# mLSTM exponents from broadcast row parts and a ScalarE bias, with the row work spread over small steps

## The chip, the cores and the metric

The kernel runs on one core of one Trainium2 chip. The metric is the device time of one execution in microseconds (us), the median over runs; the profile of one further execution tells where the time went. The engines of the core work in parallel, each through its own queue in order: TensorE (PE in the rows; PEld is its weight load), VectorE (DVE), ScalarE (ACT), GpSimd (POOL) and SyncE (SP), which starts DMA transfers here.

## The reference, cut to what matters

One encoder layer over 2048 tokens of width 1024: three token mixers (a bidirectional mLSTM with 4 heads, a neighbourhood attention, a cross-attention into 256 memory tokens), sigmoid gates that merge them, an output projection, and an MLP of width 4096. All of it is float32. The part that the change touches is the chunk step of the mLSTM, run once forwards and once on the flipped sequence:

```python
b = jnp.cumsum(lf, axis=-1)                       # lf: log of the forget gate
d_log = jnp.where(tril, b[..., :, None] - b[..., None, :] + ig[..., None, :], -jnp.inf)
inter = b + m_st[..., None]
m_t = jnp.maximum(inter, jnp.max(d_log, axis=-1))
s = jnp.einsum('bhtd,bhsd->bhts', q, k) * jnp.exp(d_log - m_t[..., None])
w_inter = jnp.exp(inter - m_t)
num = s @ v + w_inter[..., None] * (c_st @ q)     # shortened
den = jnp.sum(s, axis=-1) + w_inter * (n_st @ q)
h = num / jnp.maximum(jnp.abs(den), jnp.exp(-m_t))[..., None]
```

followed by the update of the state `c_st`, `n_st`, `m_st`. Afterwards the two directions are added, normalised per head and multiplied by a gate `og`. The exponent `d_log - m_t` is a sum of a part that hangs on the column s alone, `a = ig - b`, and a part that hangs on the row t alone, `r = b - m_t`; above the diagonal its exponential is zero.

## The kernel before, in words

The program has three phases. Phase 1 projects the input and runs the attention branches, phase 2 runs the mLSTM beside the gate products, phase 3 does the merge, the output projection and the MLP. The projections are made as three float32 passes over a high and a low part of both operands (`mm3`, L232 to L234), which makes TensorE the busiest engine. TensorE's instructions run in the order in which the code emits them; the other engines' queues are ordered by the scheduler from dependencies and priorities. All DMAs are started from the SP queue.

Phase 2 (`phase_2`, `late_gates`) emits 48 gate groups. One is 24 matmuls into one `mm` buffer of PSUM (there are two), over weights `ws` split by ScalarE (L176, high part) and VectorE (L177, low part); ScalarE evicts it with a Tanh. After each sixth matmul `tick()` lets the generator `ml_stream` (L623) run one step, so a gate group has four ticks. The stream idles for `START_2` = 20 ticks and then goes in slots of four ticks. The slots alternate between direction 0 (chunks 0 to 15) and direction 1 (15 to 0); a chunk is 128 tokens (64 in the reference; the sum is the same). Each slot starts one chunk of its direction (`ml_chunk`) and steps up to four that are under way, by the table `when`. A chunk's first step starts its loads; the next makes the decay matrix `de`; then come scores, state update, denominators, `h`, and in the second half of each direction the normalisation and the transposes for the output.

Ahead of each four chunks of a direction stands `ml_block`, in one piece: it loads the gate rows `ig` and `lf` of 512 tokens for 4 heads from DRAM, forms the running sum (L749) and the running maximum (L753) by two scans on VectorE, then `a`, `r`, the decay `w` (stored to DRAM), and four transposes of the maximum on TensorE (L772) whose exponential `em` is needed for the denominator. Heads lie on 4 partitions per direction (0 to 3 and 32 to 35). For the exponents, `a` and `r` are split into a rounded high part (ScalarE copies, L759 and L762) and a low part (VectorE, L760 and L763), kept in `at` and `rp`.

Per chunk, GpSimd spreads `rp` over the four heads with a 0/1 pattern `bd` (L806, into `rd`); one TensorE product of `at` and `rd` gives a + r for 4 heads x 128 x 128 in PSUM (L809, into a buffer of the pool `mx`); ScalarE takes its exponential as `de` in one pass (L811), and GpSimd masks it. The scores (L827, two `mx` buffers) are multiplied with `de` to `pt` on VectorE (L829) and copied to `sk` on ScalarE (L831), for the other direction's later use; the keys are transposed (L838, `mx`) and weighted to `kw` (L844), `qw` is made on GpSimd (L848), the state update uses one `mx` buffer (L871, read by `C`, L877), the denominators are taken at L882, and the output transposes at L904 use one more (read by `hm`, L907). The PSUM of phase 2 is two `mm`, four `pn` and two `mx` buffers; a tag without a pool of its own, as `tr`, comes out of `mx`.

## Time and profile before

| | |
|---|---|
| median of 3 runs (lowest to highest) | 2985.45 us (2985.35 to 2986.06) |
| the profiled execution's own time, its span | 2988.64 us, 2986.9 us |
| busy: TensorE, VectorE, ScalarE, GpSimd | 97%, 69%, 40%, 8% of the span |
| mean granted TensorE clock | 0.995 |
| HBM traffic over the span | 211 GB/s |

The times of the engines overlap. The span runs from the first to the last instruction of the profiled execution, and the view in order of time counts from its start. Idle time of an engine that is not the one the others wait for costs nothing; idle time of TensorE in a stretch lengthens it. Phase 2 lies roughly between 965 and 1365 us.

### The profile page before, as it was taken

What the parts mean: (1) busy time and instruction counts of PE and PEld (TensorE: products, weight loads), DVE (VectorE), ACT (ScalarE), POOL (GpSimd) and SP (SyncE); (2) the same over time, 40 slices, a digit from 0 to 9 for tenths busy, and PEclk for the clock granted to TensorE, in tenths of its full rate; (3) what the DMA queues carried; (4) which work ended last, traced back from release to release, by engine and by line L of the source; (5) the groups of instructions that cost most, each with busy time, mean ns of one, the idle gap of its engine ahead of it and who ended that gap; (6) DMA issues with size and microseconds to landing.
All of it is one profiled execution on the core that took longest, in us unless ns stands there. A gap on an engine that the chain in (4) does not pass through costs nothing.

```text
span 2986.9 us, 41900 instructions
## 1 busy us (share of the span) xinstructions
PE 2910.6 (97%) x15028; PEld 2374.8 (80%) x15028; DVE 2070.4 (69%) x3557; ACT 1195.1 (40%) x2198; POOL 237.1 (8%) x389
## 2 busy tenths in 40 slices
PE   8999999999999899999999999999999999999999
PEld 6778788878877677778888888888878888888887
DVE  6676775567654765674769888666676888885666
ACT  6454654344543333342233333543312433344331
POOL 3020210011000322330000000000000000000000
PEclk9999999999999999999999999999999999999999
DMA  8776777867799667789535444766874444466655
GB/s 276 225 253 202 231 227 240 266 217 217 240 283 307 195 199 234 240 276 315 183 110 169 155 152 155 275 191 224 268 235 128 137 155 151 154 226 225 195 182 165
DMA packets 341712, 632.97 MB, mean 212 GB/s; under 512 B 29344, under 2 KB 151008, under 8 KB 341504
## 3 DMA queue, kind: packets, MB, share of 16 engines
q1 hardware_dynamic: 341504, 630.30, 65.4%
q8 instruction: 118, 1.93, 0.3%
q14 instruction: 90, 0.74, 0.1%
HBM read 453.63 MB, written 176.55 MB: 211 GB/s over the span
## 4 chain that ended last, share of the span: by engine, by line
PE 55%; DVE 2%; DMA 2%; issue 1%; ACT 0%; POOL 0%; SPq 0%; DVEq 0%; ACTq 0%; POOLq 0%
PE mm L232 18%; PE mm L234 18%; PE mm L233 18%; PE mm L1339 0%; DVE h L900 0%; DMA og<-s_o 0%; DMA wr<-in_w_units_dram 0%; DMA hf<-s_hf 0%; DVE ev L1495 0%; ACT hf L896 0%; POOL rs L325 0%; DVE acc L1488 0%; DVE ws L177 0%; DVE h L888 0%; DMA X<-s_a 0%
## 5 line engine op out<-in xcount | busy, mean ns | idle before, releaser
L232 PE MATMUL mm<-X,ws 128*128 128x512 f32 x1152 | 448.5, 389 | 0.0
L234 PE MATMUL mm<-X,ws 128*128 128x512 f32 x1152 | 448.2, 389 | 0.0
L233 PE MATMUL mm<-X,ws 128*128 128x512 f32 x1152 | 448.1, 389 | 0.0
L232 PE MATMUL mm<-hT,ws 128*128 128x512 f32 x896 | 375.6, 419 | 12.1 <-ACT cz L654 5.5
L177 DVE TENSOR_TENSOR ws<-wr,ws 128x1024 fp32r<-128x1024 f32 (+1 forms) x212 | 263.0, 1246 | 142.8 <-ACT ws L176 137.7
L234 PE MATMUL mm<-hT,ws 128*128 128x512 f32 x896 | 353.6, 395 | 0.0
L233 PE MATMUL mm<-hT,ws 128*128 128x512 f32 x896 | 353.4, 394 | 0.0
L233 PE MATMUL mm<-X 128*128 128x512 f32 x896 | 348.8, 389 | 2.5 <-DVE X L1462 2.5
L234 PE MATMUL mm<-X 128*128 128x512 f32 x896 | 348.7, 389 | 0.5 <-DVE X L1462 0.5
L232 PE MATMUL mm<-X 128*128 128x512 f32 x896 | 348.7, 389 | 0.4 <-ACT X L1461 0.4
L1461 ACT ACTIVATE X<-X 128x1024 fp32r<-128x1024 f32 x176 | 187.0, 1063 | 319.4 <-DMA X<-s_t 124.5
L1462 DVE TENSOR_TENSOR X<-X 128x1024 fp32r<-128x1024 f32 x176 | 214.3, 1224 | 132.8 <-ACT X L1461 132.0
L176 ACT ACTIVATE ws<-wr 128x1024 fp32r<-128x1024 f32 (+1 forms) x212 | 223.5, 1059 | 164.7 <-PE mm L234 91.8
L232 PE MATMUL mm<-ws,hT 128*128 128x512 f32 (+2 forms) x704 | 260.9, 371 | 9.3 <-ACT cz L654 5.1
L234 PEld LDWEIGHTS mm<-X,ws 128*128 128x128 f32 x1152 | 216.2, 188 | 45.1
L233 PEld LDWEIGHTS mm<-X,ws 128*128 128x128 f32 x1152 | 216.2, 188 | 44.9
L232 PEld LDWEIGHTS mm<-X,ws 128*128 128x128 f32 x1152 | 216.2, 188 | 44.5
L234 PE MATMUL mm<-ws,hT 128*128 128x512 f32 (+2 forms) x704 | 249.8, 355 | 1.1 <-DVE hT L434 1.1
L233 PE MATMUL mm<-ws,hT 128*128 128x512 f32 (+2 forms) x704 | 249.0, 354 | 0.3 <-DVE ws L177 0.3
L202 ACT ACTIVATE ws<-wr 128x512 fp32r<-128x512 f32 x224 | 135.3, 630 | 219.9 <-PE mm L234 139.3
L232 PEld LDWEIGHTS mm<-hT,ws 128*128 128x128 f32 x896 | 170.2, 190 | 54.1 <-issue 9.8
L234 PEld LDWEIGHTS mm<-hT,ws 128*128 128x128 f32 x896 | 169.6, 189 | 39.0
(266 smaller groups left out, 4855.3 us busy)
## 6 DMA issues: line engine op xcount, KB each, us to landing
wr<-in_w_units_dram SPq DMA_DIRECT2D x308, 512.0 KB
s_s<-u SPq DMA_DIRECT2D x32, 1024.0 KB
X<-s_s SPq DMA_DIRECT2D x64, 512.0 KB
X<-s_t SPq DMA_DIRECT2D x64, 512.0 KB
s_g<-ev SPq DMA_DIRECT2D x96, 256.0 KB
ev<-s_g SPq DMA_DIRECT2D x96, 256.0 KB
s_a<-u SPq DMA_DIRECT2D x96, 256.0 KB
X<-s_a SPq DMA_DIRECT2D x48, 512.0 KB
```

Source lines behind the costliest of these rows:

```text
L176: nc.scalar.activation(w[:, 0], raw, AF.Copy)
L177: nc.vector.tensor_tensor(w[:, 1], raw, w[:, 0].bitcast(F32), ALU.subtract)
L202: nc.scalar.activation(hi, src, AF.Copy)
L232: mm(out, lhs[0], rhs[0], start=first, stop=False)
L233: mm(out, lhs[0], rhs[1], start=False, stop=False)
L234: mm(out, lhs[1], rhs[0], start=False, stop=last)
L1461: nc.scalar.activation(hi, src, AF.Copy)
L1462: nc.vector.tensor_tensor(lo, src, hi.bitcast(F32), ALU.subtract)
```

## The change

The product of `at` and `rd` is gone, with the constants `bd`, `at`, `rd`, `rp`, the high and low parts and GpSimd's L806. The row part `r` is stored to DRAM (`s_r`) and loaded again, per chunk, as one row of 4 x 128 numbers copied to all 128 partitions (`rb`, 262 KB). The column part `a` is transposed on TensorE beside the maximum (eight transposes per block and direction in place of four) and copied by VectorE to `ac`; ScalarE forms `de` in four passes of 128 columns, one per head, with `ac` as the bias.

`ml_block` becomes the generator `ml_rows(n)`, which treats both directions' block n together. Its rows are one fixed set of five tiles for all blocks; `a`, `r` and the exponential of `w` take both directions in one instruction over 36 partitions. It goes one step per tick: loads, four empty ticks, four ticks with a scan each, one for `a`, `r` and the store of `r`, one for `w`, and one for each direction's transposes. Block 0's begins at tick 8 of the 20 (`ROWS_2`), those of blocks 1 to 3 at the slots 3, 11 and 19; a block's first chunks are due at the slots 8, 16 and 24.

```diff
@@ ml_stream
-        for _ in range(START_2):
+        rows = self.ml_rows(0)
+        for tick in range(START_2):
+            if tick >= ROWS_2:
+                next(rows, None)
             yield
...
-            if c is not None and c % 4 == (0, 3)[d]:
-                self.ml_block(d, c // 4)
+
+            if slot % 8 == 3 and slot < 24:
+                rows = self.ml_rows(slot // 8 + 1)
+            slot += 1
...
+                next(rows, None)
                 yield
@@ ml_consts
...
-        self.packs = []
+        self.pack = [t("r_" + x, [36, TB + 2 * (x == "m")]) for x in "ifbmw"]
@@ ml_block / ml_rows
+        for d, b, hs in dirs:
+            for x, name in ((lf, "lf"), (ig, "ig")):
+                nc.sync.dma_start(x[hs], self.scr[name][4 * d:4 * d + 4, b * TB:(b + 1) * TB])
+        for _ in range(4):
+            yield
+        for d, _, hs in dirs:
+            nc.vector.tensor_tensor_scan(rev(d, bs[hs]), self.reset[hs], rev(d, lf[hs]), 0.0, ALU.mult, ALU.add)
+            yield
...
         nc.vector.tensor_tensor(a, ig, bs, ALU.subtract)
-        nc.scalar.activation(at[hs], a, AF.Copy)
-        nc.vector.tensor_tensor(at[lo], a, at[hs].bitcast(F32), ALU.subtract)
         nc.vector.tensor_tensor(r, bs, cm, ALU.subtract)
-        nc.scalar.activation(rp[hs].bitcast(F32R), r, AF.Copy)
-        nc.vector.tensor_tensor(rp[lo], r, rp[hs], ALU.subtract)
...
+        for d, b, hs in dirs:
+            self.store(self.scr["r"][d][b].rearrange("c h t -> h c t"), r[hs].rearrange("h (c t) -> h c t", t=128))
+        yield
...
+        for d, b, hs in dirs:
+            yield
+            p = self.ps("mx", (128, 4, 128))
+            for c in range(4):
+                for x, col in ((cm, 0), (a, 4)):
+                    nc.tensor.transpose(p[:, c, col:col + 4], x[hs, c * 128:(c + 1) * 128], self.ident[hs, hs])
+            em, ac = self.row(f"r_em{d}", (128, 4, 4)), self.row(f"r_a{d}", (128, 4, 4))
+            nc.scalar.activation(em, p[:, :, 0:4], AF.Exp, scale=-1.0)
+            nc.vector.tensor_copy(ac, p[:, :, 4:8])
@@ ml_chunk
-        rd = self.rd[d, c % 2]
+
+        rb = self.t(f"rb{d}", [128, 4, 128], 2)
+        nc.sync.dma_start(rb, self.scr["r"][d][b][cc].unsqueeze(0).to_broadcast([128, 4, 128]))
...
-        nc.gpsimd.tensor_tensor(rd[64:100], self.bd, R["rp"][:, cs].unsqueeze(1).to_broadcast([36, 4, 128]), ALU.mult)
-        yield
-        pd = self.ps("mx", (128, 4, 128))
-        nc.tensor.matmul(pd, R["at"][:, cs], rd, start=True, stop=True)
+        yield
         de = self.t(f"de{d}", [128, 4, 128], 1)
-        nc.scalar.activation(de, pd, AF.Exp)
+        for h in range(4):
+            nc.scalar.activation(de[:, h], rb[:, h], AF.Exp, bias=R["ac"][:, cc, h:h + 1])
```

What this does to the queues is shown at three places; the numbers at the ends of names tell one use of a buffer from another. First TensorE's queue at an early chunk, from the exponents' product to the scores; `mm` is a gate group's buffer. Before:

```order
L809 MATMUL mx_11143<-rd_10774,at_10773 128x512
L232 MATMUL mm_11130<-hT,ws_10898 128x512
L233 MATMUL mm_11130<-hT,ws_10898 128x512
L234 MATMUL mm_11130<-hT,ws_10898 128x512
L232 MATMUL mm_11130<-hT,ws_10898 128x512
L233 MATMUL mm_11130<-hT,ws_10898 128x512
L234 MATMUL mm_11130<-hT,ws_10898 128x512
L827 MATMUL mx_11155<-qk_1953_11054 128x128
L827 MATMUL mx_11156<-qk_1953_11054 128x128
L827 MATMUL mx_11155<-qk_1953_11054 128x128
L827 MATMUL mx_11156<-qk_1953_11054 128x128
```

and after (the scores' line is now L825):

```order
L232 MATMUL mm_11100<-hT,ws_10868 128x512
L233 MATMUL mm_11100<-hT,ws_10868 128x512
L234 MATMUL mm_11100<-hT,ws_10868 128x512
L232 MATMUL mm_11100<-hT,ws_10868 128x512
L233 MATMUL mm_11100<-hT,ws_10868 128x512
L234 MATMUL mm_11100<-hT,ws_10868 128x512
L825 MATMUL mx_11126<-qk_1952_11044 128x128
L825 MATMUL mx_11127<-qk_1952_11044 128x128
L825 MATMUL mx_11126<-qk_1952_11044 128x128
L825 MATMUL mx_11127<-qk_1952_11044 128x128
```

The product ahead of the gate matmuls has gone; the gate matmuls and the scores keep their order.

Second, TensorE's queue at the chunk in whose scores the first transposes of a later block now follow. Before, six gate matmuls follow the scores:

```order
L233 MATMUL mm_11354<-hT,ws_10997 128x512
L234 MATMUL mm_11354<-hT,ws_10997 128x512
L827 MATMUL mx_11403<-qk_1988_11245 128x128
L827 MATMUL mx_11404<-qk_1988_11245 128x128
L827 MATMUL mx_11403<-qk_1988_11245 128x128
L827 MATMUL mx_11404<-qk_1988_11245 128x128
L232 MATMUL mm_11354<-hT,ws_10997 128x512
L233 MATMUL mm_11354<-hT,ws_10997 128x512
L234 MATMUL mm_11354<-hT,ws_10997 128x512
L232 MATMUL mm_11354<-hT,ws_10997 128x512
L233 MATMUL mm_11354<-hT,ws_10997 128x512
L234 MATMUL mm_11354<-hT,ws_10997 128x512
```

and after, where `r_m` is the running maximum and `r_i` holds `a`:

```order
L825 MATMUL mx_11401<-qk_1986_11222 128x128
L825 MATMUL mx_11402<-qk_1986_11222 128x128
L825 MATMUL mx_11401<-qk_1986_11222 128x128
L825 MATMUL mx_11402<-qk_1986_11222 128x128
L769 MATMUL mx_11411<-ident,r_m 128x4
L769 MATMUL mx_11411<-ident,r_i 128x4
L769 MATMUL mx_11411<-ident,r_m 128x4
L769 MATMUL mx_11411<-ident,r_i 128x4
L769 MATMUL mx_11411<-ident,r_m 128x4
L769 MATMUL mx_11411<-ident,r_i 128x4
L769 MATMUL mx_11411<-ident,r_m 128x4
L769 MATMUL mx_11411<-ident,r_i 128x4
```

The eight transposes moved in directly behind the four score matmuls, alternating between the two row tiles.

Third, VectorE's queue where the second block's row work begins; `ws` is the low part of a weight unit, `r_b` and `r_m` are the scans' outputs, `pt` and `kw` belong to chunks. Before:

```order
L829 TENSOR_TENSOR pt_1968_11154<-mx_11155,de_1967_11145 128x2x128
L829 TENSOR_TENSOR pt_1968_11154<-mx_11156,de_1967_11145 128x2x128
L749 SCALAR_TENSOR_TENSOR r_b_11647<-reset,r_f_11646 4x512
L844 TENSOR_TENSOR kw_1972_11176<-mx_11171,de_1967_11145 128x256
L753 SCALAR_TENSOR_TENSOR r_m_11648<-r_f_11646,r_m_11648,r_i_11645 4x512
L177 TENSOR_TENSOR ws_11126<-wr_11125,ws_11126 128x8x128
L754 COPY carry<-r_m_11648 4x1
L758 TENSOR_TENSOR r_i_11645<-r_i_11645,r_b_11647 4x512
L749 SCALAR_TENSOR_TENSOR r_b_11647<-reset,r_f_11646 4x512
L761 TENSOR_TENSOR r_b_11647<-r_b_11647,r_m_11648 4x512
L760 TENSOR_TENSOR at_10783<-r_i_11645,at_10783 4x512
L829 TENSOR_TENSOR pt_1982_11220<-mx_11221,de_1981_11211 128x2x128
```

and after:

```order
L742 SCALAR_TENSOR_TENSOR r_b<-reset,r_f 4x512
L177 TENSOR_TENSOR ws_11055<-wr_11054,ws_11055 128x8x128
L742 SCALAR_TENSOR_TENSOR r_b<-reset,r_f 4x512
L748 SCALAR_TENSOR_TENSOR r_m<-r_f,r_m,r_i 4x512
L749 COPY carry<-r_m 4x1
L748 SCALAR_TENSOR_TENSOR r_m<-r_f,r_m,r_i 4x512
L827 TENSOR_TENSOR pt_1966_11125<-mx_11126,de_1965_11113 128x2x128
L827 TENSOR_TENSOR pt_1966_11125<-mx_11127,de_1965_11113 128x2x128
L749 COPY carry<-r_m 4x1
L751 TENSOR_TENSOR r_i<-r_i,r_b 36x512
L752 TENSOR_TENSOR r_b<-r_b,r_m 36x512
L759 TENSOR_TENSOR r_w<-r_b,r_m 4x512
```

The four scans moved from behind that chunk's `pt` to ahead of it, and the low part of a weight unit now stands between the first and the second.

## Rows read from the trace of the kernel before

**Rows 1.** The page's engine totals: busy us (share of span) x instructions.

```profile
PE 2910.6 (97%) x15028; PEld 2374.8 (80%) x15028; DVE 2070.4 (69%) x3557; ACT 1195.1 (40%) x2198; POOL 237.1 (8%) x389
```

**Rows 2.** Busy us by engine in stretches; then granted clock, DMA share, GB/s.

```profile
1000.00:1040.00 40.00, 31.20 (x142) 24.29 (x141) 29.03 (x35) 16.25 (x30) 18.32 (x12) 0.92 0.60 189
1034.00:1042.00 8.00, 7.53 (x31) 6.13 (x31) 6.52 (x12) 4.36 (x10) 1.06 (x2) 0.61 0.54 181
1080.00:1120.00 40.00, 37.11 (x221) 27.03 (x221) 28.41 (x54) 16.25 (x37) 11.84 (x15) 1.00 0.57 185
1160.00:1200.00 40.00, 37.67 (x232) 27.63 (x233) 29.18 (x59) 12.96 (x31) 12.14 (x17) 1.00 0.76 260
1200.00:1240.00 40.00, 38.83 (x223) 29.58 (x220) 26.39 (x57) 15.40 (x56) 16.81 (x25) 1.00 0.76 236
1240.00:1280.00 40.00, 38.00 (x219) 28.82 (x219) 27.16 (x59) 14.28 (x47) 14.54 (x23) 1.00 0.81 248
1280.00:1320.00 40.00, 38.30 (x221) 29.18 (x220) 29.81 (x69) 16.28 (x57) 15.81 (x21) 1.00 0.91 279
1320.00:1360.00 40.00, 37.78 (x199) 29.99 (x198) 25.13 (x58) 18.58 (x65) 7.54 (x12) 1.00 0.83 260
```

**Rows 3.** TensorE in order of time: start us, us, instruction, count.

```profile
1000.87 0.39 PE L234 MATMUL mm<-hT,ws 128*128 128x512 f32 x1
1001.19 0.41 PE L772 MATMUL mx<-ident,r_m 4*128 4x4 f32 x4
...
1001.86 0.40 PE L233 MATMUL mm<-hT,ws 128*128 128x512 f32 x1
...
1016.61 0.40 PE L809 MATMUL mx<-rd,at 100*128 100x512 f32 x1
1016.84 0.40 PE L232 MATMUL mm<-hT,ws 128*128 128x512 f32 x1
```

**Rows 4.** Order of time, all engines, 1024 to 1035; [idle before, released by].

```profile
1024.70 1.21 DVE L749 TENSOR_TENSOR_SCAN r_b<-reset,r_f 4x512 f32<-4x512 f32 x1 [4.54 <-DMA r_f<-s_lf]
...
1026.28 0.71 PE L827 MATMUL mx<-qk 64*128 64x128 f32 x8 [1.09 <-DVE kw L844]
...
1029.19 1.59 POOL L806 TENSOR_TENSOR rd<-bd,rp 36x512 fp32r<-36x512 f32 x1
1029.69 2.17 DVE L749 TENSOR_TENSOR_SCAN r_b<-reset,r_f 4x512 f32<-4x512 f32 x1
...
1033.57 0.76 DVE L829 TENSOR_TENSOR pt<-mx,de 128x256 f32<-128x256 f32 x2
...
1034.47 0.69 PE L838 MATMUL mx<-ident,qk 128*128 128x128 f32 x2 [5.89 <-ACT sk L831]
```

**Rows 5.** Groups around the mLSTM stage: busy us, mean ns, idle before.

```profile
L811 ACT ACTIVATE de<-mx 128x512 f32<-128x512 f32 x32 | 18.9, 592 | 28.2 <-PE mx L809 26.4 <-issue 1.6
L896 ACT ACTIVATE hf<-h 128x128 f32<-128x128 f32 x64 | 19.0, 300 | 26.1 <-DVE h L893 26.1
L806 POOL TENSOR_TENSOR rd<-bd,rp 36x512 fp32r<-36x512 f32 x32 | 44.9, 1406 | 56.4 <-PE mx L809 30.2 <-DVE rp L763 25.6
L772 PE MATMUL mx<-ident,r_m 4*128 4x4 f32 x32 | 3.2, 203 | 0.0
```

**Rows 6.** TensorE's waits, 1200 to 1360: us in total, times, longest us.

```profile
PE mx L871 <- DVE hm L907: 3.5, 6, 1.4
PE mx L809 <- ACT sm L882: 0.7, 1, 0.7
PE tr L904 <- DVE C L877: 0.6, 1, 0.6
```

**Rows 7.** The page's costliest groups: the two halves of a weight unit.

```profile
L177 DVE TENSOR_TENSOR ws<-wr,ws 128x1024 fp32r<-128x1024 f32 (+1 forms) x212 | 263.0, 1246 | 142.8 <-ACT ws L176 137.7
L176 ACT ACTIVATE ws<-wr 128x1024 fp32r<-128x1024 f32 (+1 forms) x212 | 223.5, 1059 | 164.7 <-PE mm L234 91.8
```

**Rows 8.** DMA queue, 960 to 1400: packets, MB, share of 16 engines.

```profile
q1 hardware_dynamic: 90450, 105.91, 74.6%
```

More of the change, by code (lines that the diff above doesn't have):

```diff
@@ L305, in scratch @@
             w=[[d(f"s_w{i}{b}", [4, TB]) for b in range(NB)] for i in range(2)],
+            r=[[d(f"s_r{i}{b}", [4, 4, 128]) for b in range(NB)] for i in range(2)],
             hm=[d(f"s_hm{b}", [128, 2, 4, TB]) for b in range(NB)],
@@ L623, in ml_stream @@
     def ml_stream(self):
-        for _ in range(START_2):
+        rows = self.ml_rows(0)
+        for tick in range(START_2):
+            if tick >= ROWS_2:
+                next(rows, None)
             yield
+        slot = 0
         dirs = [list(range(16)), list(range(15, -1, -1))]
@@ L735, in ml_logsig, with ml_rows @@
         self.store(view(self.scr["lf"]), l)
-    def ml_block(self, d, b):
+    def ml_rows(self, n):
         nc = self.nc
-        n = b if d == 0 else 3 - b
-        hs = slice(32 * d, 32 * d + 4)
-        if d == 0:
-            self.packs.append({x: self.row("r_" + x, (36, TB + (x == "m")), bufs=1) for x in "ifbmw"})
-        P = {x: y[hs] for x, y in self.packs[n].items()}
-        ig, lf, bs, m, w = (P[x] for x in "ifbmw")
-        nc.sync.dma_start(ig, self.scr["ig"][4 * d:4 * d + 4, b * TB:(b + 1) * TB])
-        nc.sync.dma_start(lf, self.scr["lf"][4 * d:4 * d + 4, b * TB:(b + 1) * TB])
-        rev = (lambda x: x[:, ::-1]) if d else (lambda x: x)
-        nc.vector.tensor_tensor_scan(rev(bs), self.reset[hs], rev(lf), 0.0, ALU.mult, ALU.add)
-        cm, ce = (m[:, 1:], m[:, 0:1]) if d == 0 else (m[:, :TB], m[:, TB:])
-        carry = self.carry[hs]
-        nc.vector.tensor_copy(ce, carry)
-        nc.vector.tensor_tensor_scan(rev(cm), rev(lf), rev(ig), ce, ALU.add, ALU.max)
-        nc.vector.tensor_copy(carry, m[:, TB:] if d == 0 else m[:, 0:1])
-        lo = slice(32 - 32 * d, 36 - 32 * d)
-        at, rp = self.at[d, n % 2], self.rp[d, n % 2]
-        a, r = ig, bs
@@ new lines, in ml_rows @@
+        ig, lf, bs, m, w = self.pack
+        cm, a, r = m[:, 1:TB + 1], ig, bs
+        dirs = [(d, n if d == 0 else 3 - n, slice(32 * d, 32 * d + 4)) for d in range(2)]
+        rev = lambda d, x: x[:, ::-1] if d else x
+        for d, b, hs in dirs:
[6 more added lines that the diff above has]
+            yield
@@ L758, in ml_block @@
+        for d, _, hs in dirs:
+            ce = m[hs, 0:1] if d == 0 else m[hs, TB + 1:TB + 2]
+            carry = self.carry[hs]
+            nc.vector.tensor_copy(ce, carry)
+            nc.vector.tensor_tensor_scan(rev(d, cm[hs]), rev(d, lf[hs]), rev(d, ig[hs]), ce, ALU.add, ALU.max)
+            nc.vector.tensor_copy(carry, m[hs, TB:TB + 1] if d == 0 else m[hs, 1:2])
+            yield
         nc.vector.tensor_tensor(a, ig, bs, ALU.subtract)
-        nc.scalar.activation(at[hs], a, AF.Copy)
@@ L768, in ml_block @@
-        nc.scalar.activation(w, w, AF.Exp)
-        self.store(self.scr["w"][d][b], w)
-        p = self.ps("mx", (128, 4, 128))
-        for c in range(4):
-            nc.tensor.transpose(p[:, c, 0:4], cm[:, c * 128:(c + 1) * 128], self.ident[hs, hs])
-        em = self.row(f"r_em{d}", (128, 4, 4))
-        nc.scalar.activation(em, p[:, :, 0:4], AF.Exp, scale=-1.0)
-        self.rows[d, b] = dict(at=at, rp=rp, em=em)
+        for d, b, hs in dirs:
+            self.store(self.scr["r"][d][b].rearrange("c h t -> h c t"), r[hs].rearrange("h (c t) -> h c t", t=128))
@@ new lines, in ml_rows @@
+        yield
+        for d, _, hs in dirs:
+            ms = (m[hs, 0:TB] if d == 0 else m[hs, 2:TB + 2]).rearrange("p (c t) -> p c t", t=128)
+            ms = ms[:, :, 0:1] if d == 0 else ms[:, :, 127:128]
+            nc.vector.tensor_tensor(w[hs].rearrange("p (c t) -> p c t", t=128), r[hs].rearrange("p (c t) -> p c t", t=128),
+                                    ms.to_broadcast([4, 4, 128]), ALU.add)
+        nc.scalar.activation(w, w, AF.Exp)
+        for d, b, hs in dirs:
+            self.store(self.scr["w"][d][b], w[hs])
@@ new lines, in ml_rows @@
+        for d, b, hs in dirs:
+            yield
[6 more added lines that the diff above has]
+            nc.vector.tensor_copy(ac, p[:, :, 4:8])
+            self.rows[d, b] = dict(em=em, ac=ac)
```

24 lines of the change are left out of this document (3 added, 21 removed).

## The prediction

> **What bounds the kernel now.** I read the engine totals first, then the stage that the change touches, cut into 40 us pieces, then the waits and the order of time at the places where TensorE stands still. TensorE is busy for 97% of the span [rows 1], so time is won only by taking work from it or by closing a gap in it. The mLSTM stage fills the pieces of rows 2, 1000 to 1360, and some 30 us ahead of them: 32 chunk steps (16 chunks, two directions) woven into the gate products. The pieces show where TensorE stands: 40.00 - 31.20 = 8.8 us in 1000 to 1040, 2.9 in 1080 to 1120, 2.3 in 1160 to 1200, and 1.2 + 2.0 + 1.7 + 2.2 = 7.1 in 1200 to 1360. The first three pieces are the ones in which the row work of a new block of four chunks is done (`ml_block`). In 1034 to 1042 the granted clock is 0.61: after the long stop TensorE ran for a while at the lower of its two levels, 1.2 instead of 2.4 GHz, which cost 8.0 x 0.39 = 3.1 us more.
>
> The longest stop in order of time [rows 4]: the DVE runs block 1's row work from 1024.70 on, first a sum scan of 1.21 us; the score matmuls of L827 wait 1.09 us for the `kw` queued behind it; then row work holds the DVE until `pt` (L829) starts at 1033.57. `pt` frees one of the two `mx` buffers in PSUM, and L838, which needs one, starts at 1034.47 after 5.89 us idle. This is VectorE's queue, not TensorE's work.
>
> **The change, part by part.**
>
> TensorE's work. One matmul per chunk (L809) goes. From its start to the next start is 16.84 - 16.61 = 0.23 us [rows 3] (its 0.40 us overlaps the next): 32 x 0.23 = **-7.4 us**, all of it on the path. The row transposes double: per block and direction 4 more for `a`. Around today's four, L234 at 1000.87 and L233 at 1001.86 are 0.99 us apart [rows 3], where two steps of about 0.23 would be 0.46, so four cost 0.53. Most of that is the change to another kind of matmul and back; four in a row take 0.41 from first start to last end with 0.20 for one (L772 in rows 5), so a further one costs about 0.07. The eight groups get 4 x 0.07 = 0.28 each, **+2.2 us** (no less; up to 8 x 0.53 = 4.2 if alternating between the two row tiles costs like a new group). Together **-5.2**.
>
> Block 0 and block 1. The first block's rows are now worked from tick 8 on and no longer pass through ScalarE twice, and its transposes stand two ticks earlier; the gate evictions that queued behind those ScalarE copies go through. In VectorE's new order block 1's row work starts earlier, but three of its four scans still stand behind a weight half (`ws_11055`) and ahead of chunk 0's `pt`. I time that from the end of the gate group whose eviction precedes that weight half on ScalarE: eviction 0.59 (the 128x512 pass of L811 [rows 5]), weight copy 1.06 and lower half 1.25 [rows 7], three scans at 1.21 [rows 4] = 3.6, and from the start of `pt` to L838 34.47 - 33.57 = 0.90 [rows 4]: 7.4 us. TensorE has 24 matmul steps of 0.23 and the scores, 0.71 [rows 4], before it needs the buffer: 6.2. So I expect a stop of 1.2, and with about 0.1 a piece for three hand-overs **1.5 us**; bounds 0 and today's 5.9. A stop of that size did not lower the clock: 1080 to 1120 has 2.9 us idle and a clock of 1.00 [rows 2]. So 8.8 + 3.1 becomes 1.5: **-10.4**.
>
> The same scan that takes 1.21 us took 2.17 at 1029.69, while GpSimd ran L806 (from 1029.19, 1.59 us) [rows 4]. The Trainium skill, "SBUF — State Buffer", section "Who interferes with whom", says that VectorE and GpSimd lock a shared port: an instruction of VectorE with two SBUF inputs and one of GpSimd that reads SBUF wait for each other whole. The trace agrees, with the 0.96 us above. By the rule the scans can still be held by the masking and `qw` that stay on GpSimd; one such hold for each of three scans would make the stop 1.5 + 3 x 0.96 = 4.4 us, which is the milder form of rival B. By the sum it stays 1.5, because L806, 32 x 1.41 us [rows 5], is the part that goes.
>
> Blocks 2 and 3. Idle today 2.9 + 2.3 = 5.2. The new row work does the two directions in one instruction where it can (`a`, `r`, the exponential of `w`), drops the four split and copy steps per direction, and lies 12 ticks long from slot 3 (11, 19) on, five slots before it is needed. What is left of delay behind it I put at 0.3 to 0.5 a block, 0.8 in all: -4.4. Against it stands a new wait: for blocks 1 and 2 the first transposes stand directly behind the scores of a chunk, which hold both `mx` buffers, where today six gate matmuls lie between. They wait for `pt` and the copy beside it, 0.90 by rows 4, say 1.0 each: +2.0 (bounds 0 and 2 x 5.9). Block 3 meets chunks whose scores are loaded, so none there. Together **-2.4**.
>
> The second half, 1200 to 1360, has 7.1 us idle. Of it 3.5 + 0.7 + 0.6 = 4.8 [rows 6] are waits for an `mx` buffer. They come from the ring of two: in this half each chunk step takes three of them in turn (exponents, state update, transposes), so the update waits for transposes of just before. With the exponents' buffer gone two remain, and each has one to itself: **-4.8**. The rest waits for `h`, which the change does not shorten on TensorE's side.
>
> Loads. Each chunk adds a load of 128 copies of a 2 KB row, 262 KB, 32 x 0.262 = 8.4 MB. In the stage 105.91 MB took 74.6% of 16 engines for 440 us [rows 8]: by bytes 0.262/105.91 x 0.746 x 440 = 0.81 us a load, by packets 128/90450 x 328 = 0.46. In the first half, with a DMA share of 0.57 to 0.76 [rows 2], this fits: a chunk step takes some 10 us (32 in those 360 us, less a start of 20), so the share rises by 0.08. In the second half the share is 0.76, 0.81, 0.91 and 0.83 and would reach about 1.0 in the third piece. There loads of `hf` and `og` will land later and hold `h`: I take **+3.0 us**, bounds 0 and 6. The load itself is asked for up to four slots ahead (two buffers a direction) and its store five slots ahead; only block 0 has the two close together, some 4 ticks, and there ScalarE's first `de` waits with a gate eviction behind it, which has one whole gate group (24 x 0.23 = 5.5 us) to spare.
>
> ScalarE. Four passes of 128 columns instead of one of 512: 4 x 0.30 (L896) against 0.59 (L811) [rows 5], +0.61 x 32 = 19.5 us. ScalarE has 13 to 19 us of work per 40 us [rows 2], so this is hidden; the passes wait for no matmul now, and the mask ends sooner, not later. If that cover were gone it would cost up to 0.61 a chunk. The GpSimd, constant and carry edits leave TensorE alone.
>
> Sum: -5.2 - 10.4 - 2.4 - 4.8 + 3.0 = **-19.8 us**. The profiled execution took 2988.64 us (span 2986.9 and 1.7 around it), 3.2 above the median of the runs; the terms are differences, so I take them from the median: 2985.45 - 19.8 = **2965.7 us**.
>
> **Rivals.**
> *B, VectorE's queue stays the bound at block 1.* The scans stand ahead of chunk 0's `pt` in the new order too; if they start late, or are held by GpSimd as the scan at 1029.69 was [rows 4], the matmul that follows the scores stops for today's 5.9 instead of 1.5, and the clock falls again (3.1): 2965.7 + 4.4 + 3.1 = 2973.2. For it: the order itself. Against: the row loads are asked for earlier.
> *C, the DMA engines become the bound of the second half.* They then give back all that the ring waits and the removed matmuls bring there: 4.8 + 16 x 0.23 = 8.5 instead of the 3.0: 2965.7 + 5.5 = 2971.2. For it: 0.91 [rows 2].
> *D, the row work disappears wholly.* No stop at block 1 (1.5), no remainder (0.8), no wait of the transposes (2.0), no cost of the loads (3.0): 2965.7 - 7.3 = 2958.4. For it: VectorE loses half of its row instructions and GpSimd's lock.
> *E, the broadcast is dear, and the kernel is slower.* All 128 packets of a load read one 2 KB row of DRAM. No row has such a packet by itself. If a load cost 2.8 us of all engines instead of 0.81, 2.0 more, the full second half would lengthen by 16 x 2.0 = 32 us: 2965.7 + 32 - 3 = 2994.7. It turns the sign from (19.8 + 3)/16 + 0.81 = 2.2 us a load on. Against it: the loads of `wb`, which copy one row to 64 partitions, twice per chunk, hold no TensorE wait of rows 6.
> *F, the new form does not help.* What is won at block 1 comes back as waits of ScalarE for late row parts, since `de` stands ahead of gate evictions: about 16 chunks by 1 us, 2982.
>
> **How the numbers follow.** Forecast 0.50, D 0.12, B 0.15, C 0.11, E 0.06, F 0.06. The range takes in D with the forecast's lower bounds (2956) and B with C at their bounds (2973.2 + 5.5 = 2979); E and F and a little of the tails, 0.17, stay outside. A difference of 0.2% (6 us) is about what a measurement of this kernel can tell from no change. Faster by more than that: forecast, D, B and C, 0.88; within it: F, 0.06; slower: E, 0.06.
>
> **What would show it.** Right: TensorE has no L809; 1000 to 1040 has under 3 us idle and a clock of 1.00; in 1200 to 1360 no wait of the state update for `hm`; the first transposes of blocks 1 and 2 wait about 1 us for the scores' copies; the DMA share of the second half near 0.95. Wrong: a stop over 4 us with a clock below 1.00 after it (B); a DMA share at 1.0 with waits for `hf`, `og` and `h` of over 8 us on TensorE (C, E); `de` waiting for its row parts in most chunks (F).

## The result, and the profile after

The changed kernel takes 2991.2 us (median of 20 runs, 2984.68 to 3001.82), the kernel before 2985.56 us (20 runs, 2980.64 to 2991.54); the ratio is 1.002, interval 1.0012 to 1.0027. It was forecast to gain 19.8 us and lost 5.6. The profiled execution took 2989.85 us, with a span of 2988.1 us. Its page begins as [rows 1] does:

```profile
PE 2910.7 (97%) x15028; PEld 2374.4 (79%) x15028; DVE 2033.4 (68%) x3524; ACT 1204.6 (40%) x2274; POOL 181.2 (6%) x348
```

Stretches of it, with the columns of [rows 2]:

```profile
1000.00:1040.00 40.00, 37.74 (x203) 29.29 (x201) 23.80 (x41) 17.75 (x45) 7.62 (x11) 1.00 0.75 233
1080.00:1120.00 40.00, 38.53 (x232) 28.53 (x232) 24.78 (x52) 16.45 (x45) 6.83 (x12) 1.00 0.71 225
1160.00:1200.00 40.00, 36.24 (x222) 26.96 (x221) 23.60 (x59) 13.67 (x43) 7.35 (x15) 1.00 0.85 275
1200.00:1240.00 40.00, 40.00 (x236) 30.75 (x236) 24.86 (x55) 16.36 (x61) 8.06 (x16) 1.00 0.82 254
1240.00:1280.00 40.00, 34.62 (x182) 25.05 (x181) 23.41 (x58) 15.55 (x59) 9.88 (x19) 0.96 0.81 256
1280.00:1320.00 40.00, 35.78 (x192) 25.85 (x190) 23.71 (x52) 16.55 (x57) 8.94 (x16) 0.96 0.88 272
1320.00:1360.00 40.00, 35.90 (x171) 28.14 (x168) 24.51 (x57) 18.87 (x68) 7.56 (x12) 0.96 0.87 272
```

The start came out nearly as forecast: 1000 to 1040 has 40.00 - 37.74 = 2.3 us idle where it had 8.8, at a clock of 1.00. In 1080 to 1120 TensorE stands 1.5 us (2.9 before), but in 1160 to 1200 3.8 (2.3 before). Then 1200 to 1240 is full, and from 1240 on TensorE stands for 5.4, 4.2 and 4.1 us, together 13.7 where it was 5.9. The clock there is 0.96 where it was 1.00: after some of these stops TensorE ran for a while at the lower of its two levels, 1.2 instead of 2.4 GHz, which costs 3 x 40 x 0.04 = 4.8 us more (0.79 in 1268 to 1276, for one, behind 2.4 us of waits between 1265 and 1268). So the gain was made and given back in the second half of the same stage.

I follow this by the start of each gate group (24 matmuls of L232 to L234), counted from the first that runs without the mLSTM. What the changed kernel had gained on the kernel before since then: 8.7 us at group 10 (1054.6 us before), 11.3 at group 24 (1203.1), 13.5 at group 29 (1250.8); at group 39 (1347.4) it had lost 1.7. In the ten slots from 29 to 39 it lost 15.2. TensorE's waits from 1200 to 1360 (in all, times, longest), and the one that stands for `h` in the same stretch of the kernel before:

```profile
PE tr L902 <- DVE h L898: 9.1, 14, 1.7
PE tr L902 <- DVE sm L883: 4.6, 5, 1.5
```

```profile
PE tr L904 <- DVE h L900: 2.0, 2, 1.7
```

Against [rows 6] the waits for an `mx` buffer are gone, as forecast, and waits of the output transposes for `h` have taken their place (L883, the reciprocal of the denominators, stands between two parts of L898 in VectorE's queue). What `h` waits for is read in order of time over one slot:

```profile
1290.13 0.32 SPq L849 DMA_DIRECT2D og<-s_o  x1
...
1290.55 0.38 SPq L855 DMA_DIRECT2D hf<-s_hf  x1
...
1291.02 0.93 SPq L101 DMA_DIRECT2D s_hm<-hm  x2
...
1293.61 0.69 DVE L851 SCALAR_TENSOR_TENSOR og<-og,gml 128x512 f32<-128x512 f32 x1 [0.48 <-DMA og<-s_o]
...
1294.22 1.22 DVE L177 TENSOR_TENSOR ws<-wr,ws 128x1024 fp32r<-128x1024 f32 x1
...
1295.35 0.68 DVE L891 TENSOR_TENSOR h<-h,hf 128x512 f32<-128x512 f32 x1
...
1296.17 0.60 ACT L904 ACTIVATE hm<-tr 128x512 fp32r<-128x512 f32 x1 [2.87 <-DMA s_hm<-hm]
...
1296.67 0.30 ACT L894 ACTIVATE hf<-h 128x128 f32<-128x128 f32 x1
...
1298.03 0.19 POOL L325 TENSOR_SCALAR rs<-sm 128x4 f32<-128x4 f32 x1 [1.85 <-ACT sm L880]
...
1298.30 1.01 POOL L326 TENSOR_TENSOR rs<-rs,mhalf 128x4 f32<-128x4 f32 x1
...
1299.35 0.35 DVE L898 SCALAR_TENSOR_TENSOR h<-h,rs,og 128x128 f32<-128x128 f32 x1 [1.10 <-POOL rs L326]
...
1299.84 0.56 PE L902 MATMUL tr<-ident,h 128*128 128x128 f32 x2 [0.86 <-DVE sm L883]
...
1300.61 0.60 DVE L898 SCALAR_TENSOR_TENSOR h<-h,rs,og 128x128 f32<-128x128 f32 x2
...
1301.24 0.32 SPq L849 DMA_DIRECT2D og<-s_o  x1
```

This is a closed loop, 1301.24 - 1290.13 = 11.1 us a turn, where the slots without a stop took 9.16 before. SP may load `og` only when `h` (L898) has read the one buffer that a direction has for it; from 1240 to 1320 SP waits for that longest of all:

```profile
SPq L849 <- DVE h L898: 26.1, 7, 4.2
```

From the load, two paths lead to the squares (L894). One goes over VectorE: L851, which multiplies `og`, waits for the load to land, and in VectorE's queue the weight half L177 and the sum L891 of the chunk before, which the squares need, stand behind it; the sum ends at 1295.35 + 0.68 = 1296.03. The other goes over SP and ScalarE: behind the load of `og` stands the store of `hm`, for which ScalarE's next copy `hm` (L904) waits 2.87 us, and the squares stand behind that copy; they begin at 1296.67, 0.64 us later. From the squares both go on over the root on GpSimd to `h`, and with it to the next load of `og`.

The kernel before has the same links, partly in another order. ScalarE's queue in the second half before, then after (`hf` is where the squares of a chunk go, `sm` the denominators, `ev` a gate group):

```
L906 ACTIVATE hm_13934<-tr_13929 128x512
L176 ACTIVATE ws_13851<-wr_13850 128x8x128
L811 ACTIVATE de_2617_13992<-mx_13990 128x512
L896 ACTIVATE hf_2588_13862,sm_13903<-h_2597_13899 128x128 x4
...
L904 ACTIVATE hm_13953<-tr_13948 128x512
L894 ACTIVATE hf_2553_13768,sm_13810<-h_2561_13806 128x128 x4
L880 ACTIVATE sm_13912<-pn_13882 128x2
L880 ACTIVATE sm_13912<-pn_13883 128x2
L809 ACTIVATE de_2606_14010<-rb_2573_13860,r_a_2388_13040 128x128 x4
```

The chunks that are squared ahead of the first to the seventh of the sixteen copies `hm` are 2, 3, 4, 5, 6, 7, 8 before and 2, 3, 4, **4, 5, 6, 7** after: from the fourth copy on, the squares stand one `hm` later. I call this the slip. In VectorE's queue, of the first 13 chunks' sums, 9 stand behind the next chunk's `og` before, and all 13 after.

So the loop is not new. What is new is that TensorE feels it. Let the lead of a chunk be the time from the end of its last L898 to the start of its first output transpose. For the third to the thirteenth chunk of the second half it is, in us:

| | |
|---|---|
| before | 12.7, 10.9, 8.3, 6.6, 5.7, 5.6, 5.7, 3.6, 4.4, 5.1, 0.6 |
| after | 6.3, 4.1, 1.3, 0.1, 0.1, 0.4, 0.1, 0.1, 0.1, 0.1, 0.1 |

From the fourth to the thirteenth chunk `h` comes every 10.9 us before and every 11.6 after (ends of L898), while a slot without a stop takes TensorE 9.16 and 8.9. Before, the loop was already slower than TensorE, and the lead just lasted. In the changed kernel TensorE comes sooner, the lead is used up at the sixth chunk, and from there on the loop sets the pace.

### The profile page after: what moved, and what is told of

Its sections match the earlier page's. It is cut to its first block, busy times and chain, and to the rows that moved or that the text cites. A ratio compares the mean times of both kernels' runs of the same rounds, so it can differ in the third digit from the quotient of the medians.

```text
span 2988.1 us, 41876 instructions
## 1 busy us (share of the span) xinstructions
PE 2910.7 (97%) x15028; PEld 2374.4 (79%) x15028; DVE 2033.4 (68%) x3524; ACT 1204.6 (40%) x2274; POOL 181.2 (6%) x348
## 4 chain that ended last, share of the span: by engine, by line
PE 55%; DMA 3%; DVE 1%; SPq 1%; ACT 0%; issue 0%; POOL 0%; DVEq 0%; ACTq 0%
PE mm L232 18%; PE mm L233 18%; PE mm L234 18%; DMA rb<-s_r 1%; PE mm L1337 0%; DMA wr<-in_w_units_dram 0%; DMA hT<-s_hT 0%; DMA s_hm<-hm 0%; SPq L101 0%; PE pn L860 0%; DVE ev L1493 0%; DVE h L898 0%; DMA wb<-s_w 0%; DVE acc L1486 0%; DVE h L886 0%
## 5 line engine op out<-in xcount | busy, mean ns | idle before, releaser
L232 PE MATMUL mm<-X,ws 128*128 128x512 f32 x1152 | 448.5, 389 | 0.0
L234 PE MATMUL mm<-X,ws 128*128 128x512 f32 x1152 | 448.2, 389 | 0.0
L232 PE MATMUL mm<-hT,ws 128*128 128x512 f32 x896 | 376.3, 420 | 12.6 <-DMA hT<-s_hT 6.1
L177 DVE TENSOR_TENSOR ws<-wr,ws 128x1024 fp32r<-128x1024 f32 (+1 forms) x212 | 258.6, 1224 | 153.8 <-ACT ws L176 150.9
L234 PE MATMUL mm<-hT,ws 128*128 128x512 f32 x896 | 354.6, 396 | 0.0
L234 PE MATMUL mm<-X 128*128 128x512 f32 x896 | 349.4, 390 | 0.1
L232 PE MATMUL mm<-X 128*128 128x512 f32 x896 | 349.2, 390 | 0.0
L232 PE MATMUL mm<-ws,hT 128*128 128x512 f32 (+2 forms) x704 | 259.9, 369 | 6.0 <-ACT zif L529 3.5
L232 PEld LDWEIGHTS mm<-X,ws 128*128 128x128 f32 x1152 | 216.3, 188 | 45.1
L234 PEld LDWEIGHTS mm<-X,ws 128*128 128x128 f32 x1152 | 216.2, 188 | 44.8
L234 PE MATMUL mm<-ws,hT 128*128 128x512 f32 (+2 forms) x704 | 249.8, 355 | 2.0 <-DVE hT L435 2.0
L232 PEld LDWEIGHTS mm<-hT,ws 128*128 128x128 f32 x896 | 170.7, 191 | 54.1 <-issue 8.7
L234 PEld LDWEIGHTS mm<-hT,ws 128*128 128x128 f32 x896 | 170.3, 190 | 39.1
```

The lines of the kernel that those rows point to most:

```text
L177: nc.vector.tensor_tensor(w[:, 1], raw, w[:, 0].bitcast(F32), ALU.subtract)
L232: mm(out, lhs[0], rhs[0], start=first, stop=False)
L234: mm(out, lhs[1], rhs[0], start=False, stop=last)
```

## Experiments

Theory 1 is this loop, at first read over the store of `hm` alone. Its rivals: the added loads fill the DMA engines (2), and `de` waits for its row parts with ScalarE's queue behind it (3). In brackets stands what each run had gained by its profile at groups 10, 24, 29 and 39, counted as above (changed kernel: 8.7, 11.3, 13.5, -1.7).

**e1: two buffers for `hm`.**

```diff
-        hm = self.t("hm", [128, 2, 4, 128], 1, F32R)
+        hm = self.t("hm", [128, 2, 4, 128], 2, F32R)
```

> The changed kernel with two buffers in place of one for hm, the output copy of a chunk. Theory 1 (a loop of waits in the second half): ScalarE's copy hm (L904) waits for the store of the last hm; SP has that store behind the load of og, which waits for h of L898; h waits for the squares (L894), which stand behind hm in ScalarE's queue. One turn takes the 11.3 us of a slot there, where 9.2 are needed. With a second buffer hm no longer waits for its store, the ten slots between 1240 and 1340 us take about 9.2 to 9.5 us each, and the kernel about 2972 us (18 to 20 less than the 2991 of the changed kernel). Theory 2 (the DMA engines are full in the second half) and theory 3 (de waits for its row parts and holds ScalarE's queue): no change, 2991 us.

Measured: 2980.27 us, ratio 0.9987 (0.9977 to 0.9997) [8.7, 11.7, 13.9, 7.9]. Half of what theory 1 forecast: the wait of `hm` is gone, but slots still take about 10.5 us, because the path over VectorE holds. One slot of e1 in order of time:

```profile
1284.81 0.32 SPq L849 DMA_DIRECT2D og<-s_o  x1
...
1287.66 0.69 DVE L851 SCALAR_TENSOR_TENSOR og<-og,gml 128x512 f32<-128x512 f32 x1
...
1288.27 1.22 DVE L177 TENSOR_TENSOR ws<-wr,ws 128x1024 fp32r<-128x1024 f32 x1
...
1289.40 0.68 DVE L891 TENSOR_TENSOR h<-h,hf 128x512 f32<-128x512 f32 x1
...
1290.17 0.31 ACT L894 ACTIVATE hf<-h 128x128 f32<-128x128 f32 x1 [2.88 <-DVE h L891]
...
1292.86 0.35 DVE L898 SCALAR_TENSOR_TENSOR h<-h,rs,og 128x128 f32<-128x128 f32 x1 [1.10 <-POOL rs L326]
...
1295.21 0.32 SPq L849 DMA_DIRECT2D og<-s_o  x1
```

From `og` to `og` 10.4 us, now over L851 (VectorE stood 0.14 us before it, until `og` had landed), the weight half and the sum L891 alone; ScalarE waits 2.88 for that sum. The slip is still there. Between the start of a sum and its first square lie 0.8 to 2.4 us in the changed kernel (fifth to thirteenth chunk) and 0.7 to 0.8 here: that is what the copy `hm` and its wait add to a turn.

**e2: a quarter of the added loads.**

```diff
-        nc.sync.dma_start(rb, self.scr["r"][d][b][cc].unsqueeze(0).to_broadcast([128, 4, 128]))
+        nc.sync.dma_start(rb[0:32], self.scr["r"][d][b][cc].unsqueeze(0).to_broadcast([32, 4, 128]))
```

> The changed kernel, but each load of the row parts fills 32 partitions in place of 128, a quarter of its bytes and packets; the other 96 partitions hold zeros from one memset, so the exponents there are wrong. The queues of all engines stay as they are. Theory 1 (loop of waits by hm, og and the squares): the load of the row parts is no link of the loop, 2989 to 2991 us, hm still waits 3 to 5 us per slot. Theory 2 (DMA engines full): three quarters of the added 8.4 MB go, the second half gets its 9.2 us per slot, about 2972 us. Theory 3 (de waits for its row parts): they land 1 to 3 us earlier, de waits less, 2980 to 2985 us.

Measured: 2991.07 us, 1.002 (1.001 to 1.003) [8.8, 13.7, 15.4, -3.9]. Rivals 2 and 3 fall for the second half: `de` waits less, and `hm` waits as long as ever. At group 24 this kernel is 2.4 us ahead of the changed one, and the loop takes that back too. Waits of e2 between 1240 and 1320 (in all, times, longest):

```profile
ACT hm L907 <- DMA s_hm<-hm: 36.1, 7, 6.2
ACT de L812 <- DMA rb<-s_r: 7.9, 6, 1.7
```

The same two in the changed kernel:

```profile
ACT hm L904 <- DMA s_hm<-hm: 30.7, 7, 5.6
ACT de L809 <- DMA rb<-s_r: 12.6, 6, 3.1
```

**e3: two buffers for `og`,** which take away what SP waits for.

```diff
-            og = self.t(f"og{d}", [128, 512], 1)
+            og = self.t(f"og{d}", [128, 512], 2)
```

> The changed kernel with two buffers per direction in place of one for og. The load of og no longer waits for h, so SP passes on at once to what stands behind it (hf, the store of hm, the loads of the next chunk). Theory 1: the loop is cut at another link, the slots of 1240 to 1340 us take 9.2 to 9.5 us, about 2972 us or a little less since the row parts also land earlier. Theory 2: 2991 us. Theory 3: the row parts are asked for several us earlier, so 2972 to 2980 us as well; e1 tells it from theory 1.

Measured: 2969.69 us, 0.9943 (0.9931 to 0.9956) [7.2, 10.6, 12.8, 17.2]. The load of `og` no longer waits for the `h` of the chunk just before. The slip is gone too (2, 3, 4, 5, 6, 7, 8), and so are most of the stops, in the stretches of e3:

```profile
1240.00:1280.00 40.00, 39.61 (x222) 29.72 (x220) 27.46 (x68) 19.45 (x71) 11.77 (x23) 1.00 0.98 304
1280.00:1320.00 40.00, 39.19 (x213) 29.03 (x212) 26.56 (x66) 19.50 (x69) 9.49 (x16) 1.00 0.95 298
```

**e4 and e6: the same two edits in the kernel before.**

> The kernel before, with two buffers for hm; its queues stay the same but for a few places. Theory 1: in the kernel before, the squares stand one copy hm earlier in ScalarE's queue and the loop is not closed, so nothing changes: 2984 to 2986 us. Rival: hm's single buffer bounds the second half of both kernels, then this one gains too, 2978 to 2981 us.

> The kernel before, with two buffers per direction for og, so that SP's queue does not stop at its load. Theory 1: in the kernel before, the second half waits for mx buffers (4.8 of 7.1 us) and little for the load of og, so it gains 0 to 3 us: 2982 to 2985 us; the gain of 22 us that the same edit brought in the changed kernel belongs to the change's loop. Rival: SP's stop at og bounds the second half of both kernels: then this one gains 6 us or more, 2979 us or less.

Measured: e4 2985.55 us, 1.0 (0.9991 to 1.0008); e6 2986.13 us, 0.9994 (0.9984 to 1.0004). Neither gains, so the 11 and 22 us that these buffers bring belong to the changed kernel, where the lead is gone. In e6 the last ten slots run without the `mx` waits of [rows 6], which I had not expected: by its profile they gain 6.6 us, after 5.8 us lost up to group 29 (one stop of 2.6 us at 1228 among them). So the loop was not free in the kernel before either.

**e9: no buffer, only the order of two loads.**

```diff
         if second:
+            early = c >= 10 if d == 0 else c < 6
+            if early:
+                hf = self.t(f"hf{d}", [128, 4, 128], 1)
+                nc.sync.dma_start(hf, self.scr["hf"][c].rearrange("t (h e) -> t h e", h=4))
             og = self.t(f"og{d}", [128, 512], 1)
...
-        if second:
+        if second and not early:
```

> The changed kernel with no further buffer; only the load of hf is asked for one step earlier, ahead of the load of og in SP's queue (for the chunks whose hf is long stored). The squares then come two or more copies hm earlier in ScalarE's queue, so h no longer waits for a store that SP holds behind og. Theory 1 (a loop of waits through SP's queue): the slots of 1240 to 1340 us fall from 11.3 us to about 9.7, as with two buffers for og, and the kernel to about 2970 us. Rival (the shortage is of buffers or of DMA time, not of order): no change, 2991 us.

Measured: 2970.02 us, 0.9948 (0.9936 to 0.996) [8.7, 13.0, 12.6, 17.9]. With the two loads the other queues changed as well. The squares now stand ahead of the copies (2, 3, 4, 6, 7, 8, 9), and from the fifth chunk on the sum stands ahead of the next chunk's `og` in VectorE's queue (L895 and L855 in this kernel; a stretch in order of time):

```profile
1275.34 0.68 DVE L895 TENSOR_TENSOR h<-h,hf 128x512 f32<-128x512 f32 x1
...
1275.94 0.69 DVE L855 SCALAR_TENSOR_TENSOR og<-og,gml 128x512 f32<-128x512 f32 x1
...
1276.46 0.44 SPq L853 DMA_DIRECT2D og<-s_o  x1
```

Both paths of the loop are open. `h` comes every 8.3 us (fourth to thirteenth chunk), its lead is 8.0 to 13.1 us from the fifth chunk to the thirteenth, and from 1256 on a slot takes 8.9 us. A stretch of e9:

```profile
1280.00:1320.00 40.00, 40.00 (x230) 31.39 (x228) 29.76 (x70) 18.97 (x70) 11.38 (x19) 1.00 1.00 325
```

TensorE does not stand at all, beside a DMA share of 1.00.

**e16: `og` asked for by GpSimd instead of SP.**

```diff
-            nc.sync.dma_start(og, self.scr["og"][b][cs])
+            nc.gpsimd.dma_start(og, self.scr["og"][b][cs])
```

> The changed kernel, with one word changed: the load of og is asked for by GpSimd in place of SP. No buffer is added. Theory 1: GpSimd now waits for h of L898, and SP's queue goes on with hf, the store of hm and the next chunk's loads; the loop is open, the slots of 1240 to 1340 us take about 9.7 us in place of 11.3, and the kernel about 2970 us. If what counts is only the time that SP spends on issuing (0.32 us for this load, 14 times), the gain is below 5 us: 2986 to 2991 us. If GpSimd's wait holds back its own roots and masks, the time stays at 2985 to 2995 us with GpSimd's waits in place of SP's.

Measured: 3000.49 us, 1.0046 (1.0029 to 1.0062). The third case: the wait moved to GpSimd's queue, with the masks and roots behind it, and the loop closed again through the landing of `og` (L851 stands ahead of L891 on VectorE). There is no slip in this kernel, so the loop does not need it; the one buffer for `og`, and the sum behind its multiplication, are common to the changed kernel, e1, e2, e13 and this one. Waits of e16 between 1200 and 1340:

```profile
POOL og L849 <- DVE h L898: 28.7, 10, 3.4
DVE og L851 <- DMA og<-s_o: 20.0, 11, 3.4
```

The Trainium skill, "DMA: Bandwidth & Descriptors", section "Issuing engines are not separate DMA queues", says that starting DMAs on several engines saves only the time to start them. Here that agrees, no gain (16 x 0.32 us was all to be saved); what e9 shows beside it is that the order of two loads on one issuer, with what it moved in the other queues, was worth 21 us.

**e5, e12 and e13: the halves of the change.** e5 has the small steps with the old exponents (`ml_rows` fills `at` and `rp`, four transposes, L806 to L811 as before). e12 has the new exponents with the row work in one piece; e13 is e12 with only the row loads five slots early.

```diff
-            if slot % 8 == 3 and slot < 24:
-                rows = self.ml_rows(slot // 8 + 1)
+            if slot % 8 == 0 and slot < 32:
+                for _ in self.ml_rows(slot // 8):
+                    pass
...
-                next(rows, None)
```

> Half of the change alone: the row work in small steps as in the changed kernel, but the exponents in the old form (high and low parts, GpSimd's product rd, TensorE's product into an mx buffer, one pass of ScalarE), and four transposes per block and direction. In ScalarE's queue the squares keep their place of the kernel before, ahead of the next hm. Theory 1 (the new form's gain in the second half is lost to the loop of waits, which needs the squares one hm later): the block stops of the first half shrink, about 10 us, and the second half stays at the 9.2 to 10.6 us a slot of before: about 2975 us, so half of the change alone beats the whole. Rival: the second half is lost because the row work came early (the earlier chunk steps meet the loads of the second half): then this one too loses 15 us after 1240, about 2990 us.

> The other half of the change alone: the exponents in the new form (loaded row parts, bias on ScalarE, eight transposes), but the row work of a block in one piece at the slot of its first chunk, as before, both directions together. Theory 1: the block stops of the kernel before come back at the start of each block (VectorE's row work ahead of pt, TensorE's transposes behind it), 10 to 15 us more than the changed kernel in the first half; in ScalarE's queue the squares slip back by one hm only from the seventh copy on, in place of the fourth, so of the second half's 16 us about 6 are not lost: 2993 to 2999 us. Rival: the exponents' form is what helped the first half, and the small steps did nothing: 2985 to 2988 us.

> As e12 (new exponents, row work of a block in one piece), but the block's row loads are asked for five slots ahead, as in the changed kernel. If the stop of 18.5 us at block 3 in e12 came from SP's queue, where the row loads stood behind the load of og, it goes. The squares now stand behind one hm more from the fifth copy on, so the loop of the changed kernel comes back in the second half (about 11.3 us a slot from 1250 us on, some 14 us lost). First half: if the new form carries the gain, 20 to 23 us ahead of the kernel before at 1190 us, as in e12; if the small steps carry it, 10 or less. Sum: 2980 to 2986 us in the first case, 2990 to 2997 in the second.

Measured: e5 2992.03 us, 1.002 (1.001 to 1.0029) [-8.5, -4.5, -4.6, -4.9]; e12 2985.18, 0.9995 (0.9985 to 1.0005) [13.5, 18.5, -1.5, 2.7]; e13 2994.29, 1.0025 (1.0016 to 1.0034) [7.1, 7.6, 3.6, -13.2]. e5 missed: its second half stays even, as theory 1 says, but by group 10 it has lost 8.5 us, where gate evictions stand behind ScalarE's high parts, which wait for the scans. TensorE at the longest such stop:

```profile
1018.72 0.79 PE L232 MATMUL mm<-hT,ws 128*128 128x512 f32 x1 [6.15 <-ACT ev L600]
```

e12 missed as well, with the best first half of these and one stop of 18.48 us at block 3. TensorE and SP in order of time:

```profile
1226.87 0.26 PE L766 MATMUL mx<-ident,r_i 4*128 4x4 f32 x1 [18.48 <-DVE r_i L748]
...
1219.18 0.33 SPq L846 DMA_DIRECT2D og<-s_o  x1
...
1221.29 0.33 SPq L735 DMA_DIRECT2D r_i<-s_ig  x1
```

Its row load (L735) stood behind the load of `og` (L846) in SP's queue. After that stop its slots take 8.9 us with one buffer for `og`, but not because the loop is open: the stop leaves a lead of 33.4 us at the third chunk, and as `h` comes more slowly than TensorE, 0.4 us of it is left at the thirteenth. With the row loads early it shrinks to 3.36 us in e13, the slip is there (from the fifth copy on), and the second half loses 16.8 us between groups 29 and 39: the loop of the changed kernel again, without the small steps.

**e14, e7, e8, e10, e11, e15: what is left once the loop is cut.** All have two buffers for `og`. e14 is e13 otherwise; the others are the changed kernel: e7 moves the row transposes of blocks 1 to 3 to ticks in which no chunk takes `mx` buffers, e8 deals PSUM out as `mm=2, pn=3, mx=3`, e10 has three buffers for `v`, e11 is e10 with one PSUM buffer lent to `mx` in the first half and to `pn` in the second; e15 is e14 with the edits of e11.

> As e13, with two buffers per direction for og: the loop is cut, the second half takes about 9.7 us a slot. If the new form alone carries the first half, about 2962 to 2966 us, 4 to 8 us less than e3 (the changed kernel with two buffers for og, 2969.7), so the small steps cost a little; if the small steps carry it, 2975 us or more.

> The changed kernel with two buffers for og, and the row transposes of blocks 1 to 3 moved from the ticks in which a chunk takes mx buffers for scores and keys to the first tick of the next two slots of four, where only the products into pn stand. If the waits of 1.04 us in front of them are waits for the scores' copies (ScalarE's sk), as rows of TensorE say, they go: four of about 1.0, and 2965 to 2966 us against 2969.7. If they come from VectorE's or ScalarE's backlog, they move along and the time stays 2969 to 2970 us.

> The changed kernel with two buffers for og, and PSUM's eight buffers of the stage dealt out as 2 mm, 3 pn and 3 mx in place of 2, 4 and 2. If the small stops that are left in the first half (1.5, 1.0, 1.9, 1.0, 1.0, 0.8 us before scores, keys and row transposes) are waits for a free mx buffer, most of the 7.3 us go: 2963 to 2966 us. If a third pn is too few (a slot takes two, and h of the slot before must have been read), TensorE waits at the products into pn in every slot and the time rises above 2975 us.

> The changed kernel with two buffers for og and three in place of two for v. With two for og a slot of the second half takes 9.67 us though TensorE hardly stops; the kernel before with the same edit takes 9.13. Reading: GpSimd's fill of the ones column of v (L796) waits for the state update to free a buffer, 31.9 us in all, with the root rs (L325) queued behind it, then h (L898) and TensorE's transposes (L902), which run 0.26 us apart in place of 0.11. If so, a slot falls to 9.1 to 9.2 us and the kernel by 4 to 6 us to about 2965. If VectorE's own queue sets the pace of h, nothing changes: 2969 to 2970 us.

> As the last one, and one PSUM buffer is lent: in the first half it makes three mx buffers, in the second half four pn buffers (with three of each, the first half lost its small stops and the second half waited for pn in every slot). Expected: 6 to 7 us less than the kernel with two buffers for og and three for v, about 2958 us; at least below 2964 even if the buffers for v bring nothing.

> As e14, with three buffers for v and the lent PSUM buffer of e11. If the small steps only cost, 2952 to 2957 us, less than the 2960 of e11; if they hide what is left of the row work, 2960 to 2966 us.

Measured: e14 2970.6 us, 0.9947 (0.9935 to 0.996), the same as e3, so with the loop cut the small steps neither gain nor cost. e7 2968.07, 0.9938 (0.9924 to 0.9952): the waits ahead of the row transposes, two of 1.05 in e3 where I had counted four, are gone from the trace, but in time e3 and e7 can't be told apart. e8 2987.71, 0.9998 (0.9989 to 1.0008) [11.6, 21.6, 14.2, 0.9]: both halves of the expectation at once: hardly a stop in the first half, and in the second this wait of TensorE (1200 to 1340):

```profile
PE pn L860 <- DVE h L886: 20.0, 10, 4.2
```

e10 2966.56, 0.9939 (0.9927 to 0.9951): GpSimd still waits 23.1 us to fill `v`, and the slots still take 9.6 to 10; why is open. (In e3 too the lead is 0.1 us from the seventh to the twelfth chunk: `h` still sets the pace there, at 9.7 us.) e11 **2959.97 us, 0.9913 (0.99 to 0.9925)** [11.6, 23.0, 25.2, 28.1], the best of all, 0.9% below the kernel before. e15 2963.59, 0.9918 (0.9905 to 0.9932), not to be told from e11.

## Why the prediction was wrong

- *TensorE's work, -5.2: right as far as the rows show.* Gate groups with a chunk step and no stop take 9.53 us in the first half where they took 9.80, and 8.89 (e9) where they took 9.16: 0.27 a slot for 0.23. The alternating transposes follow each other by 0.06 to 0.08, for 0.07 (TensorE in order of time, here and below):

```profile
1040.32 0.22 PE L769 MATMUL mx<-ident,r_m 4*128 4x4 f32 x1 [1.04 <-ACT sk L829]
...
1040.40 0.20 PE L769 MATMUL mx<-ident,r_i 4*128 4x4 f32 x1
...
1040.46 0.20 PE L769 MATMUL mx<-ident,r_m 4*128 4x4 f32 x1
```

- *Blocks 0 and 1, -10.4: right.* The clock did not fall, and 8.8 us became 2.3, of which 0.7 belongs to the first transposes of the next term. The stop forecast as 1.5 us at the matmul behind the scores is 1.54, by the chain that was summed (the three scans took 1.22, 1.27 and 1.27):

```profile
1017.46 0.44 PE L836 MATMUL mx<-ident,qk 128*128 128x128 f32 x2 [1.54 <-ACT sk L829]
```

- *Blocks 2 and 3, -2.4: wrong, about +3.1.* From group 10 to 24 TensorE stands 7.3 us where it stood 5.2, and ahead of that the first transposes of block 1 wait 1.04. This wait and the same of block 2 came as forecast (1.0 each). Two other waits were missing in the sum: that of the scores for the state update to leave `mx`, and one for `hT`, the input of the next gate groups, which the kernel before does not have there (waits of TensorE from 1040 to 1200):

```profile
PE mx L825 <- DVE C L875: 3.3, 3, 1.5
PE mm L232 <- DMA hT<-s_hT: 2.9, 2, 1.7
```

- *The second half, -4.8: wrong, and with it the sign.* The step that failed is "The rest waits for `h`, which the change does not shorten on TensorE's side". The waits for `mx` went, as forecast. But `h` was left as it had been, with no term for its own pace: it came every 10.9 us before and hid behind a lead, which the sum spent without counting it. With TensorE sooner and `h` every 11.6 us, the transposes' wait for `h`, 2.0 us in 1200 to 1360 before, became 9.1 + 4.6. With the chunk's product gone, forecast for groups 24 to 39 was 4.8 + 15 x 0.23 - 3.0 = 5.3 us of gain; the trace has 13.0 of loss. The stretches show 7.8 us more of standing and 4.8 of lower clock; how the rest divides they do not show. The reading of the `mx` waits was not the whole cause either: in e6 they go with a second buffer for `og`, though each chunk still takes three `mx` buffers in turn and there are two. Cutting the loop (e3, e9) gives 2970, inside the range and 4 us from the forecast; but these are other kernels, and in the sum the errors of blocks 2 and 3 (+5.5) and of the loads (-3.0) partly cancel, which is luck.
- *The loads, +3.0 in the second half: not seen there.* e2 takes three quarters of them away and gains nothing while the loop holds, and e9 runs at its fastest at a DMA share of 1.00. In the first half they may cost something: in e2 one of the two waits for `hT` is gone, and it is 2.4 us ahead at group 24, in one profile of each. The queue's bytes in 960 to 1400 rose by 9.3 MB, for 8.4 reckoned, against [rows 8]:

```profile
q1 hardware_dynamic: 95654, 115.23, 81.5%
```

- *ScalarE, hidden: right.* Four passes take 1.28 us where 1.20 was taken. One lasts 0.393. The Trainium skill, "ScalarE: Activation LUTs", section "What ACT_TABLE_LOAD costs", gives 280 ns and 0.833 ns a column with a bias per partition, by estimate 387 ns for 128 columns; the trace agrees.
- *The rivals.* None was the loop. C had the place and a part of the size (what the second half gains is given back) with the wrong cause; half of its sign came, over 8 us of waits for `h` on TensorE, but at a DMA share of 0.81 to 0.88 and not 1.0. F's wait is in the trace (12.6 us of ScalarE from 1240 to 1320); in e2 it is 7.9 and the time is the same.

What stays open: why the scheduler moved the copy ahead of the squares and more sums behind `og`; how much of the 0.7 us by which the turn grew is due to each, since no run moves one of these orders alone; and about 4 us between the profiles (span +1.2) and the medians (+5.6), of which the runs' own spread of 17 us is the likely part, not a shown one.
